# HGRN products moved from GpSimd to VectorE, operand tiles placed anew, and the opening, norm factors and row copies reordered

## The chip, the cores and the metric

The kernel runs on one core of a Trainium2 chip. The metric is the time of one execution on the device in microseconds (us); the median of several runs is compared. A difference is measured against the same runs of the kernel before.

## What is computed

The reference passes 256 tokens of 1024 features through two networks, one after the other, all in float32. The first is one block: a norm, a mixer with four branches and gates, a norm, a feed-forward, and a final norm. The second has two layers: a norm, HGRN, a feed-forward; a norm, an LRU mixer, a feed-forward; and a final norm. Cut to what matters here:

```
h = rmsnorm(x, norm_mix);  x = x + hybrid_mixer(h, ...)
h = rmsnorm(x, norm_ffn);  x = x + (silu(h @ w_gate) * (h @ w_up)) @ w_down
x = rmsnorm(x, norm_final)
x = x + hgrn2_mixer(rmsnorm(x, ...), ...);  x = x + swiglu_2(rmsnorm(x, ...), ...)
x = x + rglru_mixer(rmsnorm(x, ...), ...);  x = x + swiglu_2(rmsnorm(x, ...), ...)
x = rmsnorm(x, norm_final_2)

hgrn2_mixer: q = silu(proj_q);  f = lb + (1 - lb) * sigmoid(fl);  k = (1 - lb) * sigmoid(-fl)
             S_t = diag(f_t) S_{t-1} + k_t v_t^T;  o_t = S_t^T q_t     (8 heads of 128)
```

Here `lb` is a softmax over two rows of a parameter, the floor of the forget gate.

## The kernel before

**Matmuls.** Every dense product is done in three passes (`mm3`, line 152). Each operand is split into a high and a low part: `split` (line 99) casts a tile to the reduced form on ScalarE (line 100) and takes the difference on VectorE (line 101). The three passes are high by high (L154), and the two mixed ones (L155, L156). Weights come by DMA into `raw`, four tiles of 1 MB that SyncE's queue fills, and are split into `whi` and `wlo`, 1024 columns at a time. Activations, transposed, are split into `hh` and `hl` (the normed input of each stage), `ah` and `al` (the inner width of a feed-forward), `yh` and `yl` (branches), `oh` and `ol` (HGRN's output), `uh` and `ul` (LRU).

There are two forms of product. `gemm_a` (line 158) keeps a 128x128 piece of the activations stationary and streams up to 512 weight columns past it; so do the feed-forwards. `gemm_b` (line 185) keeps a 128x128 piece of the weights stationary and streams the 256 tokens past it; it serves where the output is wanted transposed, in the mixer, HGRN and LRU. A feed-forward (`swiglu`, line 316) runs over 2816 inner columns, five blocks of 512 and one of 256, for gate and up, and then over the 22 blocks of `ah` for the way down.

**What sets the order.** Each engine runs its instructions in one order, which a scheduler lays out from the order of the code, the readiness of the operands and priorities. `high_priority(offset=...)` moves the weight splits ahead (line 121), `issue_after` ties a piece of work behind an instruction. Tiles of a pool are reused in turn (`bufs`), and a tile's address follows from the pools and the tiles made ahead of it.

**The norm.** `norm_input` (line 199) squares a 128x512 part of `x` on ScalarE with a running sum, transposes it, scales it and splits it into `hh` and `hl`. The factor of the norm is applied later, at the eviction: `rstd` (line 232) works it out with a power on GpSimd (line 246), and `row` (line 248) makes it a row `rrow` over the tokens with two small matmuls against `dg` (line 264) and a copy on ScalarE (line 266).

**The opening.** ScalarE has the squares and casts of four parts of `x`, the casts of the first weights, and `lru_rates` (line 570), which is passed to the first feed-forward as `aside` and whose operands are parameters alone. An activation function from another set needs a table load on ScalarE (ACT_TABLE_LOAD in the trace).

**The mixer.** `skew_bias` (line 389) builds a table of relative biases with a small matmul and copies it on GpSimd's queue to `relv` and, in two large copies, to `skew` in DRAM; `bias4` reads it back for attention. `rows4` (line 437) fetches four heads' rows for the first branch, whose loop over heads (lines 644 to 656) forms `mt` from them: two operations on VectorE, an exponential on ScalarE (L651), a product on VectorE (L652), three small matmuls.

**HGRN.** At its entry (lines 1086 to 1100) the norm factors `rf` and `r` are made, `x` is scaled by `rf` on GpSimd (L1100), and the first matmuls' results are evicted as `u` = accumulator times `rrow` on VectorE (L779, L786). `hq` is `u` times its sigmoid, on GpSimd (L782); `hk` and `hf` come from ScalarE and VectorE. Then `hgrn_scores` (line 825) forms `pr` = `hq` times `hk` (L834) and its low part `pl` (L836) on GpSimd, its high part `ph` on ScalarE, sums them with a matmul of ones, and goes through seven levels with products `G` (L876) on VectorE. Meanwhile the weights of the next matmuls are split on ScalarE and VectorE.

Of the kernel before, what the change touches and what calls it, by code (L numbers as in the profile page):

```python
# [20 lines left out]
EPS = 1e-6  # L21
NEG = -1.0e30
# [52 lines left out]
class Build:  # L75
    def __init__(self, tc, a):
        self.tc, self.nc, self.a = tc, tc.nc, a
        self.uid = 0
        self.turn = 0
        self.share = 0  # L80
        self.parts = 2
        self.hold = []
        self.burst = 0
        self.wmore = None
        self.place = -1
        self.ahead = 400
# [111 lines left out]

    def norm_input(self, x, n, t, wcol, hi, lo, ss):
# [3 lines left out]
        junk = self.tmp.tile([P, 512], F32, tag="junk", name=self.nm("junk"), bufs=1)  # L203
        if ss is not None:
            nc.scalar.activation(junk, xc, AF.Square, accum_out=ss[:, t, n:n + 1])
# [26 lines left out]
    def rstd(self, ss, scale=1.0 / D):  # L232
# [3 lines left out]
        nc.vector.tensor_tensor(r, ss[:, :, 0], ss[:, :, 1], op=ALU.add)  # L236
        self.rsqrt(r, r, scale)
# [20 lines left out]
    def make_row(self, r):  # L258
        nc = self.nc
# [5 lines left out]
        rr = self.small.tile([P, S], F32, tag="rrow", name=self.nm("rrow"))  # L265
# [20 lines left out]
    def constants(self):  # L286
# [9 lines left out]

        self.cmask = c.tile([P, 3, P], F32, name="cmask")
        nc.gpsimd.memset(self.cmask, 1.0)
        for j in (0, 2):
            nc.gpsimd.affine_select(self.cmask[:, j], self.cmask[:, j], pattern=[[1, P]], compare_op=ALU.is_ge,  # L300
                                    fill=0.0, base=0, channel_multiplier=-1)
# [14 lines left out]
    def swiglu(self, hk, r, wg, g0, wu, u0, wd, x, finish, apart=0, aside=None):  # L316

        nc = self.nc
        with self.tc.tile_pool(name=self.nm("ffn"), bufs=1) as fp:
            ah = fp.tile([P, FF // P, S], F32R, name=self.nm("ah"))  # L320
            al = fp.tile([P, FF // P, S], F32R, name=self.nm("al"))
            for c0 in range(0, FF, 512):
                if c0 == 1024 and aside:
                    aside()
                n = min(512, FF - c0)
                psg, psu = self.gemm_pair(hk, wg, g0 + c0, wu, u0 + c0, n, early=c0 == 0)
                for t in range(2):
                    sg = fp.tile([P, 512], F32, tag="sg", name=self.nm("sg"), bufs=3)
                    pr = fp.tile([P, 512], F32, tag="pr", name=self.nm("pr"), bufs=3)
                    nc.scalar.activation(sg[:, :n], psg[t][:, :n], AF.Silu, scale=r[:, t:t + 1])  # L330
# [42 lines left out]
    def mixer(self, hk, r, rr, x, finish):  # L373
        nc, a, tc = self.nc, self.a, self.tc
        w_in = a["w_in"][0]
        with tc.tile_pool(name="yT", bufs=3) as ytp, tc.tile_pool(name="att", bufs=1) as at, \
# [12 lines left out]
            def skew_bias():  # L389
# [47 lines left out]
            def rows4(h0):  # L437
                rw = mp.tile([P, 4, S], F32, tag="rows", name=self.nm("rows"), bufs=1)
# [48 lines left out]

            qT2, kT2, v2 = load_qkv(3080)
# [80 lines left out]

    def lru_rates(self):  # L570
# [35 lines left out]
    def mamba(self, hk, r, rr, w_in, mp, rows4, dtc, acol, yT, then):  # L606
# [4 lines left out]
        xins = self.conv_inputs(mp, 2)  # L611
        for b in (4, 6, 0, 2):
# [9 lines left out]
        for g in range(2):  # L622
# [5 lines left out]
            nc.vector.tensor_tensor(c, ps[:, :384], self.cmask.rearrange("p a b -> p (a b)"), op=ALU.mult)  # L628
# [119 lines left out]
    def hgrn(self, hk, r, rr, x, finish):  # L748
# [3 lines left out]
        w = a["hgrn_w_in_2"][0]  # L752
        LV = (64, 32, 16, 8, 4, 2, 1)
        with tc.tile_pool(name="hgrn", bufs=1) as hp:
            lbp = self.col["hgrn_lb_2"]
            lb = hp.tile([P, 8], F32, name="lb")
            om = hp.tile([P, 8], F32, name="om")
            lt = hp.tile([P, 2, 8], F32, name="lt")
            nc.vector.tensor_tensor(lb, lbp[:, 0:8], lbp[:, 8:16], op=ALU.max)
            for i in range(2):  # L760
                nc.vector.tensor_tensor(lt[:, i], lbp[:, i * 8:(i + 1) * 8], lb, op=ALU.subtract)
            nc.scalar.activation(lt, lt, AF.Exp)
            nc.vector.tensor_tensor(om, lt[:, 0], lt[:, 1], op=ALU.add)
            nc.vector.reciprocal(om, om)
            nc.vector.tensor_tensor(lb, lt[:, 0], om, op=ALU.mult)
            nc.vector.tensor_tensor(om, lt[:, 1], om, op=ALU.mult)
            v = hp.tile([P, 2, D], F32, name="hv")
            gs = hp.tile([P, 2, D], F32, name="hg")
            oh = [hp.tile([P, 4, S], F32R, name=f"oh{g}") for g in range(2)]
            ol = [hp.tile([P, 4, S], F32R, name=f"ol{g}") for g in range(2)]  # L770
            qkf = []
            for g in range(2):
                q, k, f = (hp.tile([P, 4, S], F32, tag=n, name=self.nm(n), bufs=2) for n in ("hq", "hk", "hf"))
                qkf.append((q, k, f))
                for c in range(2):
                    h0 = 4 * g + 2 * c
                    for i, ps in enumerate(self.gemm_b(hk, w, h0 * P, 2)):
                        u = hp.tile([P, S], F32, tag="u", name=self.nm("u"), bufs=3)
                        nc.vector.tensor_tensor(u, ps, rr(), op=ALU.mult)  # L779
                        sg = hp.tile([P, S], F32, tag="sgq", name=self.nm("sgq"), bufs=2)  # L780
                        nc.scalar.activation(sg, u, AF.Sigmoid)
                        nc.gpsimd.tensor_tensor(q[:, 2 * c + i], u, sg, op=ALU.mult)  # L782
                    for i, ps in enumerate(self.gemm_b(hk, w, D + h0 * P, 2)):
                        h = h0 + i
# [241 lines left out]
    def body(self):  # L1026
        nc, a, tc = self.nc, self.a, self.tc
        with ExitStack() as es:
# [28 lines left out]
            for n in range(2):  # L1057
                for t in range(2):
                    finish(n, t)
# [103 lines left out]
```

## Time and profile before

| | us |
|---|---|
| median of 3 runs | 1179.6 |
| lowest and highest | 1176.96 and 1179.66 |
| the profiled execution | 1177.61 |
| its span, first to last instruction | 1175.9 |
| mean granted clock of TensorE | 0.992 of full speed |

The span is 1.7 us shorter than the execution's own time. The profile lists busy time by engine, groups of instructions by line and tile, and what each engine waited for; a timeline gives single instructions with their start in us from the span's start. The ends of matmuls are modelled, their starts are recorded. TensorE's granted clock is given for any stretch: 1.00 is 2.4 GHz, 0.50 is 1.2 GHz.

### The profile page before, as it was taken

What the parts mean: (1) busy time and instruction counts of PE and PEld (TensorE: products, weight loads), DVE (VectorE), ACT (ScalarE), POOL (GpSimd) and SP (SyncE); (2) the same over time, 40 slices, a digit from 0 to 9 for tenths busy, and PEclk for the clock granted to TensorE, in tenths of its full rate; (3) what the DMA queues carried; (4) which work ended last, traced back from release to release, by engine and by line L of the source; (5) the groups of instructions that cost most, each with busy time, mean ns of one, the idle gap of its engine ahead of it and who ended that gap; (6) DMA issues with size and microseconds to landing.
All of it is one profiled execution on the core that took longest, in us unless ns stands there. A gap on an engine that the chain in (4) does not pass through costs nothing.

```text
span 1175.9 us, 15771 instructions
## 1 busy us (share of the span) xinstructions
PE 1140.0 (97%) x6308; PEld 981.0 (83%) x6308; DVE 737.0 (63%) x971; ACT 615.5 (52%) x909; POOL 82.1 (7%) x87
## 2 busy tenths in 40 slices
PE   7999999999999999998999999999999879999997
PEld 7899897888888888888989878888889778888886
DVE  6976555566575555556898676555458767555552
ACT  6646647654455444446542465444446876444441
POOL 1100010000000000006520140000000000000000
PEclk9999999999999999999999999999999989999999
DMA  9785245446555555456353337554554536555440
GB/s 299 188 265 190 87 144 188 162 147 206 184 192 184 181 186 186 172 179 204 112 179 108 108 108 251 183 195 177 197 167 156 179 120 214 185 179 179 163 159 36
DMA packets 120761, 202.78 MB, mean 172 GB/s; under 512 B 4244, under 2 KB 44437, under 8 KB 120688
## 3 DMA queue, kind: packets, MB, share of 16 engines
q1 hardware_dynamic: 117264, 192.59, 50.0%
q0 software_dynamic: 2992, 8.56, 2.6%
q8 instruction: 49, 0.80, 0.3%
q10 hardware_dynamic: 432, 0.63, 0.2%
q14 instruction: 24, 0.20, 0.0%
HBM read 200.64 MB, written 4.25 MB: 174 GB/s over the span
## 4 chain that ended last, share of the span: by engine, by line
PE 84%; ACT 6%; DVE 5%; DMA 3%; issue 2%; POOLq 0%; POOL 0%; SPq 0%; ACTq 0%; DVEq 0%
PE acc L154 25%; PE acc L156 25%; PE acc L155 25%; DMA raw<-in_w_in_dram 2%; DVE wlo L101 2%; PE tp L274 2%; PE tp L865 2%; ACT whi L100 2%; PE tp L695 1%; PE tp L208 1%; DVE G L876 1%; PE tp L724 1%; PE tp L732 0%; DMA rows<-acd 0%; PE tp L731 0%
## 5 line engine op out<-in xcount | busy, mean ns | idle before, releaser
L101 DVE TENSOR_TENSOR wlo<-raw,whi 128x1024 fp32r<-128x1024 f32 (+3 forms) x364 | 444.2, 1225 | 303.5 <-ACT whi L100 296.9
L100 ACT CAST whi<-raw 128x1024 fp32r<-128x1024 f32 (+3 forms) x372 | 382.0, 1033 | 363.2 <-PE acc L156 294.3
L156 PE MATMUL acc<-whi,hl 128*128 128x512 f32 (+2 forms) x832 | 316.2, 381 | 0.0
L155 PE MATMUL acc<-wlo,hh 128*128 128x512 f32 (+2 forms) x832 | 313.7, 377 | 1.3 <-DVE wlo L101 1.3
L154 PE MATMUL acc<-whi,hh 128*128 128x512 f32 (+2 forms) x832 | 311.3, 378 | 1.3 <-ACT whi L100 1.1
L155 PEld LDWEIGHTS acc<-wlo,hh 128*128 128x128 f32 x832 | 156.4, 188 | 31.0 <-DVE wlo L101 2.4
L154 PEld LDWEIGHTS acc<-whi,hh 128*128 128x128 f32 x832 | 156.3, 188 | 28.7 <-ACT whi L100 1.9
L156 PEld LDWEIGHTS acc<-whi,hl 128*128 128x128 f32 x832 | 156.4, 188 | 28.1 <-issue 0.7
L154 PE MATMUL acc<-hh,whi 128*128 128x256 f32 (+1 forms) x496 | 142.2, 289 | 9.5 <-ACT rg L951 4.5
L156 PE MATMUL acc<-hh,wlo 128*128 128x256 f32 (+1 forms) x496 | 141.6, 287 | 1.9 <-DVE wlo L101 1.9
L155 PE MATMUL acc<-hl,whi 128*128 128x256 f32 (+1 forms) x496 | 141.8, 287 | 0.3 <-DVE hl L101 0.3
L154 PEld LDWEIGHTS acc<-hh,whi 128*128 128x128 f32 (+1 forms) x496 | 95.7, 194 | 12.7 <-ACT rg L951 4.7
L155 PE MATMUL acc<-wlo,ah 128*128 128x512 f32 x264 | 103.1, 391 | 0.0
L156 PE MATMUL acc<-whi,al 128*128 128x512 f32 x264 | 102.6, 389 | 0.0
L154 PE MATMUL acc<-whi,ah 128*128 128x512 f32 x264 | 102.5, 390 | 0.0
L156 PEld LDWEIGHTS acc<-hh,wlo 128*128 128x128 f32 (+1 forms) x496 | 95.6, 193 | 2.8 <-DVE wlo L101 2.6
L155 PEld LDWEIGHTS acc<-hl,whi 128*128 128x128 f32 (+1 forms) x496 | 95.8, 193 | 1.3 <-DVE hl L101 0.6
L156 PEld LDWEIGHTS acc<-whi,al 128*128 128x128 f32 x264 | 49.6, 188 | 10.2
L154 PEld LDWEIGHTS acc<-whi,ah 128*128 128x128 f32 x264 | 49.6, 188 | 10.1
L155 PEld LDWEIGHTS acc<-wlo,ah 128*128 128x128 f32 x264 | 49.6, 188 | 10.1
L100 ACT CAST ah<-tp 128x512 fp32r<-128x512 f32 (+1 forms) x36 | 19.8, 550 | 33.9 <-PE tp L274 33.9
L330 ACT ACTIVATE sg<-acc,rstd 128x512 f32<-128x512 f32 (+1 forms) x36 | 23.3, 648 | 20.4 <-PE acc L156 20.4
(306 smaller groups left out, 1250.8 us busy)
## 6 DMA issues: line engine op xcount, KB each, us to landing
raw<-in_ffn_w_in_dram SPq DMA_DIRECT2D x44, 1024.0 KB, 5.2
raw<-in_w_in_dram SPq DMA_DIRECT2D x33, 1024.0 KB, 5.1
raw<-in_ffn_w_out_dram SPq DMA_DIRECT2D x20, 1024.0 KB, 5.1
raw<-in_hgrn_w_in_dram SPq DMA_DIRECT2D x16, 1024.0 KB, 5.5
raw<-in_w_ffn_gate_dram SPq DMA_DIRECT2D x11, 1024.0 KB, 5.1
raw<-in_w_ffn_up_dram SPq DMA_DIRECT2D x11, 1024.0 KB, 5.2
raw<-in_w_ffn_down_dram SPq DMA_DIRECT2D x10, 1024.0 KB, 5.1
raw<-in_w_branch_dram SPq DMA_DIRECT2D x8, 1024.0 KB, 5.1
```

What stands on the lines that cost most here:

```text
L100: self.nc.scalar.copy(hi, src)
L101: (eng or self.nc.vector).tensor_tensor(lo, src, hi.bitcast(F32), op=ALU.subtract)
L154: mm(ps, sh, mh, start=start, stop=False)
L155: mm(ps, sh, ml, start=False, stop=False)
L156: mm(ps, sl, mh, start=False, stop=stop)
L208: last = nc.tensor.transpose(ps[:, j * P:(j + 1) * P], xc[:, j * P:(j + 1) * P], self.ident)
L274: nc.tensor.transpose(ps[:, j * P:(j + 1) * P], src[:, j * P:(j + 1) * P], self.ident)
L330: nc.scalar.activation(sg[:, :n], psg[t][:, :n], AF.Silu, scale=r[:, t:t + 1])
L695: nc.tensor.matmul(ps[par][:, jj * W:(jj + 1) * W], qT[pr, 2 * gi + jj, qt * P:(qt + 1) * P], kT(2 * gi + jj)[pr, :W], start=True, stop=True)
L724: nc.tensor.transpose(ps[:, i * P:(i + 1) * P], sp[:, i, b * P:(b + 1) * P], self.ident)
L865: nc.tensor.matmul(ps[:, c:c + 64], k[:, h, ts], q[:, h, ts].rearrange("p (n u l) -> p n u l", u=2, l=L)[:, :, 1], start=True, stop=True)
L876: nc.vector.tensor_tensor(G2, G[:, :, 0], G[:, :, 1], op=ALU.mult)
```

## The change

Six things change. (1) The tiles of `hh` and `hl` become 128 elements longer, and their contents start at an offset: STILL (96 elements) where they are stationary, in the feed-forwards, MOVING (16) for the three mixers. Other tiles shift with pools: `cmask` leaves the constants, `oh` and `ol` are the first in HGRN's pool, a tile of 32 elements that nobody uses is put into LRU's. (2) HGRN's `hq`, `pr` and `pl` go from GpSimd to VectorE, `x` times `rf` to ScalarE. (3) The opening writes the squares after the four transposes and casts. (4) `aside` is tied behind a silu of the first feed-forward, and the floors of HGRN (`hgrn_floors`) are worked out there too. (5) The factors of the norm and their row get a priority (`rush`). (6) In the mixer the copies to `skew` are written in two places, and `rows` has two buffers in place of one.

```diff
+STILL, MOVING = 96, 16
...
-    def new_h(self):
-        hi = [self.hp.tile([P, 4, S], F32R, tag=f"hh{n}", name=self.nm("hh")) for n in range(2)]
-        lo = [self.hp.tile([P, 4, S], F32R, tag=f"hl{n}", name=self.nm("hl")) for n in range(2)]
+    def new_h(self, place):
+
+
+        def part(tag):
+            t = self.hp.tile([P, 4 * S + 128], F32R, tag=tag, name=self.nm(tag[:2]))
+            return t[:, place:place + 4 * S].rearrange("p (k s) -> p k s", s=S)
+
+        hi, lo = ([part(f"{u}{n}") for n in range(2)] for u in ("hh", "hl"))
...
-        nc.vector.tensor_tensor(r, ss[:, :, 0], ss[:, :, 1], op=ALU.add)
-        self.rsqrt(r, r, scale)
+        with self.tc.high_priority(offset=self.rush):
+            nc.vector.tensor_tensor(r, ss[:, :, 0], ss[:, :, 1], op=ALU.add)
+            self.rsqrt(r, r, scale)
...
                 if c0 == 1024 and aside:
-                    aside()
+                    with self.tc.issue_after(last.ins):
+                        aside()
...
-                for g in range(2):
-                    nc.gpsimd.dma_start(skew[g], relv[:, g].unsqueeze(1).to_broadcast([8, P, NV]))
+                copies(0)
+
+            def copies(g):
+
+                nc.gpsimd.dma_start(skew[g], relv[:, g].unsqueeze(1).to_broadcast([8, P, NV]))
...
-                rw = mp.tile([P, 4, S], F32, tag="rows", name=self.nm("rows"), bufs=1)
+                rw = at.tile([P, 4, 384], F32, tag="sp", name=self.nm("rows"), bufs=2)[:, :, :S]
...
+            copies(1)
             qT2, kT2, v2 = load_qkv(3080)
...
-                        nc.gpsimd.tensor_tensor(q[:, 2 * c + i], u, sg, op=ALU.mult)
...
+                        nc.vector.tensor_tensor(q[:, 2 * c + i], u, sg, op=ALU.mult)
...
+            qkf = [made(g) for g in range(2)]
+            for t in range(2):
+                nc.scalar.activation(x[:, t], x[:, t], AF.Copy, scale=rf[:, t:t + 1])
...
-        nc.gpsimd.tensor_tensor(pr, q.rearrange("p h t -> p (h t)"), k.rearrange("p h t -> p (h t)"), op=ALU.mult)
-        nc.scalar.copy(ph, pr)
-        nc.gpsimd.tensor_tensor(pl, pr, ph.bitcast(F32), op=ALU.subtract)
+        nc.vector.tensor_tensor(pr, q.rearrange("p h t -> p (h t)"), k.rearrange("p h t -> p (h t)"), op=ALU.mult)
+        self.split(ph, pl, pr)
...
             xins = self.conv_inputs(lp, 4)
+            lp.tile([P, 32], F32, name="apart")
...
-            begin(col["norm_mix"])
+            begin(col["norm_mix"], MOVING)
             for n in range(2):
                 for t in range(2):
-                    finish(n, t)
+                    self.norm_input(x, n, t, state["w"], state["hi"], state["lo"], None)
+            for n in range(2):
+                for t in range(2):
+                    self.square(x[:, t, n * 512:(n + 1) * 512], state["ss"][:, t, n:n + 1])
...
-            for t in range(2):
-                nc.gpsimd.tensor_scalar(x[:, t], x[:, t], rf[:, t:t + 1], None, op0=ALU.mult)
-            begin(col["norm_ffn_2"][:, 0:8])
+            begin(col["norm_ffn_2"][:, 0:8], STILL)
```

ScalarE in the opening, before and after. `junk` is a square, `lam` and `c` belong to `lru_rates`, `whi` of 320 columns is the first weight:

```order
L584 ACTIVATE lam_3636<-lam_3636 128x8
L205 ACTIVATE junk_120,ss_104<-x 128x512
L100 CAST hh_105<-tsc_116 128x4x128
L586 ACT_TABLE_LOAD
L586 ACTIVATE c_3634<-lam_3637 128x8
L205 ACTIVATE junk_131,ss_104<-x 128x512
L100 CAST hh_105<-tsc_127 128x4x128
L205 ACTIVATE junk_142,ss_104<-x 128x512
L100 CAST whi_177<-raw_175 128x320
```

```order
L427 ACTIVATE sm<-pcol 40x1
L204 ACTIVATE junk_143,ss_100<-x 128x512
L102 CAST hh_101<-tsc_110 128x4x128
L204 ACTIVATE junk_145,ss_100<-x 128x512
L102 CAST hh_101<-tsc_119 128x4x128
L204 ACTIVATE junk_147,ss_100<-x 128x512
L102 CAST whi_173<-raw_171 128x320
```

The two activations of `lru_rates` and their table load are gone; squares and casts alternate as before.

ScalarE in the mixer, at the second pair of heads, before and after. `mt` are the exponentials, `whi` the casts of the weights:

```order
L100 CAST whi_904<-raw_898 128x1024
L100 CAST whi_962<-raw_960 128x1024
L651 ACT_TABLE_LOAD
L651 ACTIVATE mt_683<-mt_683 128x384
L651 ACTIVATE mt_691<-mt_691 128x384
L100 CAST whi_966<-raw_960 128x1024
```

```order
L102 CAST whi_903<-raw_897 128x1024
L686 ACT_TABLE_LOAD
L686 ACTIVATE mt_682<-mt_682 128x384
L686 ACTIVATE mt_690<-mt_690 128x384
L102 CAST whi_961<-raw_959 128x1024
L102 CAST whi_965<-raw_959 128x1024
```

The first cast of the next weight tile has moved behind the table load and the two exponentials. On GpSimd's queue the second `rows` now follows the first, ahead of `relv`, `skew` and the first `bias`; before, it came last of these. The matmul that `relv` waits for stands at row 227 of TensorE's order, before at 179.

VectorE in HGRN, where the first group's products begin, before and after:

```order
L779 TENSOR_TENSOR u_5114<-acc_5064,rrow_4826 128x256
L876 TENSOR_TENSOR G_5394<-hf_4757 128x512
L876 TENSOR_TENSOR G_5438<-G_5394 128x256
L876 TENSOR_TENSOR G_5466<-G_5438 128x128
L876 TENSOR_TENSOR G_5494<-G_5466 128x64
L101 TENSOR_TENSOR wlo_5199<-raw_5196,whi_5198 128x1024
L876 TENSOR_TENSOR G_5522<-G_5494 128x32
L779 TENSOR_TENSOR u_5119<-acc_5089,rrow_4826 128x256
L845 TENSOR_TENSOR hq_4755<-hq_4755,hf_4757 128x1024
L101 TENSOR_TENSOR wlo_5203<-raw_5196,whi_5202 128x1024
```

```order
L902 TENSOR_TENSOR G_5394<-hf_4783 128x512
L861 TENSOR_TENSOR pr_5367<-hq_4781,hk_4782 128x1024
L815 TENSOR_TENSOR hq_5077<-u_5140,sgq_5142 128x256
L902 TENSOR_TENSOR G_5438<-G_5394 128x256
L103 TENSOR_TENSOR wlo_5225<-raw_5222,whi_5224 128x1024
L871 TENSOR_TENSOR hq_4781<-hq_4781,hf_4783 128x1024
L812 TENSOR_TENSOR u_5145<-acc_5115,rrow_4852 128x256
L902 TENSOR_TENSOR G_5466<-G_5438 128x128
L103 TENSOR_TENSOR pl_5369<-pr_5367,ph_5368 128x1024
L103 TENSOR_TENSOR wlo_5229<-raw_5222,whi_5228 128x1024
```

`pr`, `hq` and `pl` now stand between the weight differences. At HGRN's entry ScalarE's order has the two instructions of `x` times `rf` between the first and the second cast of a weight tile, both ahead of the copy of `rrow`; before, the casts and `rrow` followed one another.

## Rows read from the trace of the kernel before

**Rows 1.** The page's first part: busy us, share of the span, instructions of each engine.

```profile
PE 1140.0 (97%) x6308; PEld 981.0 (83%) x6308; DVE 737.0 (63%) x971; ACT 615.5 (52%) x909; POOL 82.1 (7%) x87
```

**Rows 2.** Waits of TensorE, whole run: what for, us in total, times, longest.

```profile
PE acc L154 <- ACT rg L951: 5.3, 2, 4.5
PE acc L154 <- ACT uh L100: 4.0, 1, 4.0
```

**Rows 3.** Timeline of TensorE, (a) to (d): start, us, operation, tiles.

```profile
402.15 0.39 PE L154 MATMUL acc<-whi,hh 128*128 128x512 f32 x1
...
420.94 0.40 PE L155 MATMUL acc<-wlo,hh 128*128 128x512 f32 x1
...
483.03 0.40 PE L156 MATMUL acc<-whi,al 128*128 128x512 f32 x1
...
511.60 0.40 PE L156 MATMUL acc<-whi,al 128*128 128x512 f32 x1
...
672.75 0.39 PE L155 MATMUL acc<-wlo,oh 128*128 128x512 f32 x1
...
680.65 0.39 PE L156 MATMUL acc<-whi,ol 128*128 128x512 f32 x1
...
469.23 0.28 PE L154 MATMUL acc<-whi,hh 128*128 128x256 f32 x1
...
476.53 0.28 PE L156 MATMUL acc<-whi,hl 128*128 128x256 f32 x1
```

**Rows 4.** Timeline of ScalarE and TensorE in the opening; idle time before in brackets.

```profile
6.74 1.28 ACT L586 ACT_TABLE_LOAD   x1
...
9.89 0.44 ACT L100 CAST whi<-raw 128x320 fp32r<-128x320 f32 x1
...
10.39 0.43 PE L154 MATMUL acc<-hh,whi 128*40 128x256 f32 x1 [2.02 <-ACT whi L100]
```

**Rows 5.** The mixer: timelines of ScalarE and TensorE, then a window's busy times, clock.

```profile
68.55 1.05 ACT L100 CAST whi<-raw 128x1024 fp32r<-128x1024 f32 x1 [5.51 <-DMA raw<-in_w_in_dram]
...
72.08 0.43 PE L654 MATMUL tp<-xc,mt 128*128 128x64 f32 x2 [1.26 <-DVE mt L652]
...
74.30:77.40 3.10, 3.10 (x16) 3.10 (x16) 2.12 (x8) 2.19 (x4) 0.00 (x0) 0.50 0.94 302
```

**Rows 6.** Timelines of GpSimd, VectorE and TensorE at HGRN's entry.

```profile
551.99 5.68 POOL L1100 TENSOR_SCALAR x<-x,rf 128x1024 f32<-128x1024 f32 x2
...
552.12 2.05 DVE L101 TENSOR_TENSOR wlo<-raw,whi 128x1024 fp32r<-128x1024 f32 x1 [0.90 <-ACT whi L100]
...
554.57 0.38 PE L154 MATMUL acc<-hh,whi 128*128 128x256 f32 x1 [2.70 <-DVE u L779]
```

**Rows 7.** HGRN's products: timelines of VectorE and GpSimd; waits of TensorE, 555 to 612.

```profile
563.11 1.21 DVE L101 TENSOR_TENSOR wlo<-raw,whi 128x1024 fp32r<-128x1024 f32 x1
...
570.61 2.85 DVE L876 TENSOR_TENSOR G<-hf 128x512 f32<-128x512 f32 x1
...
574.84 3.44 DVE L101 TENSOR_TENSOR wlo<-raw,whi 128x1024 fp32r<-128x1024 f32 x1
...
579.77 1.75 DVE L101 TENSOR_TENSOR wlo<-raw,whi 128x1024 fp32r<-128x1024 f32 x1
...
581.52 0.68 DVE L856 TENSOR_TENSOR p<-hq,hk 128x512 f32<-128x512 f32 x1
...
598.84 2.07 DVE L876 TENSOR_TENSOR G<-hf 128x512 f32<-128x512 f32 x1
...
601.61 3.44 DVE L101 TENSOR_TENSOR wlo<-raw,whi 128x1024 fp32r<-128x1024 f32 x1
...
574.80 2.39 POOL L836 TENSOR_TENSOR pl<-pr,ph 128x1024 fp32r<-128x1024 f32 x1 [0.75 <-ACT ph L835]
...
PE acc L156 <- DVE wlo L101: 1.9, 2, 1.6
PE acc L155 <- DVE wlo L101: 0.8, 1, 0.8
```

More of the change, by code (lines that the diff above doesn't have):

```diff
@@ L85, in __init__ @@
         self.place = -1
+        self.rush = 600
         self.ahead = 400
@@ L196, in block_b, with square @@
         return ps
+    def square(self, xc, out):
+        junk = self.tmp.tile([P, 512], F32, tag="junk", name=self.nm("junk"), bufs=1)
+        self.nc.scalar.activation(junk, xc, AF.Square, accum_out=out)
     def norm_input(self, x, n, t, wcol, hi, lo, ss):
@@ L202, in norm_input @@
         xc = x[:, t, n * 512:(n + 1) * 512]
-        junk = self.tmp.tile([P, 512], F32, tag="junk", name=self.nm("junk"), bufs=1)
         if ss is not None:
-            nc.scalar.activation(junk, xc, AF.Square, accum_out=ss[:, t, n:n + 1])
+            self.square(xc, ss[:, t, n:n + 1])
         ps = self.tp()
@@ L258, in make_row, with row_of @@
     def make_row(self, r):
+        with self.tc.high_priority(offset=self.rush):
+            return self.row_of(r)
+    def row_of(self, r):
         nc = self.nc
@@ L264, in make_row @@
             nc.tensor.matmul(ps[:, t * P:(t + 1) * P], self.ones, dg, start=True, stop=True)
-        rr = self.small.tile([P, S], F32, tag="rrow", name=self.nm("rrow"))
+        rr = self.small.tile([P, S], F32, tag="rrow", name=self.nm("rrow"), bufs=1)
         nc.scalar.copy(rr, ps[:, :S])
@@ L295, in constants @@
         nc.vector.tensor_copy(self.ones_r, self.ones)
[L297 to L301, printed above, removed]
         self.col = {}
@@ L568, in mixer, with hgrn_floors @@
             gp.__exit__(None, None, None)
+    def hgrn_floors(self):
+        nc = self.nc
+        self.floors = lb, om = [self.const.tile([P, 8], F32, name=n) for n in ("lb", "om")]
+        lbp = self.col["hgrn_lb_2"]
+        lt = self.small.tile([P, 2, 8], F32, tag="lt", name="lt", bufs=1)
+        nc.vector.tensor_tensor(lb, lbp[:, 0:8], lbp[:, 8:16], op=ALU.max)
+        for i in range(2):
+            nc.vector.tensor_tensor(lt[:, i], lbp[:, i * 8:(i + 1) * 8], lb, op=ALU.subtract)
+        nc.scalar.activation(lt, lt, AF.Exp)
+        nc.vector.tensor_tensor(om, lt[:, 0], lt[:, 1], op=ALU.add)
+        nc.vector.reciprocal(om, om)
+        nc.vector.tensor_tensor(lb, lt[:, 0], om, op=ALU.mult)
+        nc.vector.tensor_tensor(om, lt[:, 1], om, op=ALU.mult)
     def lru_rates(self):
@@ L611, in mamba @@
         xins = self.conv_inputs(mp, 2)
+        cmask = mp.tile([P, 3, P], F32, name="cmask")
+        nc.gpsimd.memset(cmask, 1.0)
+        for j in (0, 2):
+            nc.gpsimd.affine_select(cmask[:, j], cmask[:, j], pattern=[[1, P]], compare_op=ALU.is_ge,
+                                    fill=0.0, base=0, channel_multiplier=-1)
         for b in (4, 6, 0, 2):
@@ L745, in attention, with hgrn @@
             self.to_T(y[:, t], yT[0], yT[1], t)
-    def hgrn(self, hk, r, rr, x, finish):
+    def hgrn(self, hk, r, rr, rf, x, finish):
         nc, a, tc = self.nc, self.a, self.tc
         w = a["hgrn_w_in_2"][0]
+        lb, om = self.floors
         LV = (64, 32, 16, 8, 4, 2, 1)
         with tc.tile_pool(name="hgrn", bufs=1) as hp:
[L755 to L766, printed above, removed]
+            oh = [hp.tile([P, 4, S], F32R, name=f"oh{g}") for g in range(2)]
+            ol = [hp.tile([P, 4, S], F32R, name=f"ol{g}") for g in range(2)]
@@ L1046, in body, with begin @@
             state = {}
-            def begin(wcol):
+            def begin(wcol, place):
                 state["ss"] = self.stat()
-                state["hi"], state["lo"], state["hk"] = self.new_h()
+                state["hi"], state["lo"], state["hk"] = self.new_h(place)
                 state["w"] = wcol
@@ L1062, in body @@
             hk = state["hk"]
-            begin(col["norm_ffn"])
+            begin(col["norm_ffn"], STILL)
             self.mixer(hk, r, rr, x, finish)
@@ L1068, in body @@
             nc.vector.tensor_tensor(wc, col["norm_final"], col["norm_mix_2"][:, 0:8], op=ALU.mult)
-            begin(wc)
+            begin(wc, MOVING)
             wfs = ExitStack()
@@ L1110, in body @@
             rr = self.row(r)
-            begin(col["norm_ffn_2"][:, 8:16])
+            begin(col["norm_ffn_2"][:, 8:16], STILL)
             self.ahead = 150
```

72 lines of the change are left out of this document (35 added, 37 removed).

## The prediction

> **What bounds the kernel now.** The first part of the profile's page comes first: TensorE is busy 97% of the span, VectorE 63%, ScalarE 52%, GpSimd 7% [rows 1]. So a microsecond off TensorE's stream is a microsecond off the end, and work on another engine counts only where TensorE waits for it. Next the waits of TensorE: the two largest groups, 5.3 us for `rg` and 4.0 us for `uh`, lie in the LRU mixer [rows 2]. The change leaves that code as it is, so they stay. What is left is small: the waits in the stretches below, and the rate of the matmuls themselves. That rate is read from starts, not from the durations of the table, which are modelled. In [rows 3] four unbroken stretches, all at the full granted clock, give the first and the last start: (a) 83 matmuls of a 512-column weight tile against stationary `hh`/`hl` in the first feed-forward, 18.79 us for 82 steps, 229.1 ns a step; (b) 127 of the same shape against `ah`/`al`, 28.57 us for 126 steps, 226.7 ns; (c) 35 against `oh`/`ol`, 7.90 us for 34 steps, 232.4 ns; (d) 63 of 256 columns against `hh`/`hl`, 7.30 us for 62 steps, 117.7 ns. Half of (b) would be 113.4 ns.
>
> **What the four stretches have in common and what not.** Instruction, shape, clock and the source of the moving tile are the same in (a), (b) and (c). The place of the stationary tile in SBUF isn't. In the program built from the kernel before, weights start at byte 416 of a 512-byte period, `ah`/`al` at 416, `hh`/`hl` at 96, `oh`/`ol` at 32. Same offset as the weights: 226.7; the two other offsets: 229.1 and 232.4. In the changed program weights, `ah`/`al`, `oh`/`ol` and the `hh`/`hl` of the feed-forwards (STILL) all start at 32; the `hh`/`hl` that serve as moving operand in the mixers (MOVING) start at 224, as far from the weights (192) as before. The trace shows the rates; that the difference of offsets is their cause is my reading, and I choose it because no other feature I could find sorts the stretches.
>
> **Part 1, the offsets.** Three feed-forwards have 480 matmuls of 512 columns each against `hh`/`hl` (five blocks of 512, 8 K-steps, 2 halves, 3 passes, gate and up): 1440 x 2.4 ns = 3.5 us. Their last blocks have 256 columns: 288 x (117.7 - 113.4) = 1.2 us. `oh`/`ol`: 96 x 5.7 = 0.5 us. Sum 5.2 us, all of it on TensorE's stream, where nothing hides it. `uh`/`ul` move from one untried offset to another (288 against 32); 96 matmuls, at most the 4.3 ns of (d) either way, 0.4 us, taken as 0. Bounds: 0 if offsets mean nothing, 5.6 with `uh`. The Trainium skill speaks against this term: "SBUF — State Buffer", section "SBUF: two separate sides", has TensorE wait for nobody at SBUF, only VectorE and GpSimd contending. By it the places would be worth nothing; the three rates in [rows 3] are not explained by it.
>
> **Part 2, the opening.** Before, ScalarE runs the logarithm of `lru_rates` between the first casts, with a table load of 1.28 us at 6.74 [rows 4]; the cast of the first weights comes at 9.89 and the first dense matmul at 10.39, after a wait of 2.02 us. `lru_rates` is now tied behind a silu in the first feed-forward, so this load leaves the opening, and 0.3 us of tiny activations with it. The order shows that the squares, though written after the casts, still stand between them, so the squares bring nothing. In the other direction the second halves of `hh` come close behind the first dense matmuls, so a few tenths may be waited for again. Taken: -1.2 us, bounds -0.3 and -1.6. The moved loads fall into the first feed-forward, beside ScalarE at half load; if that cover were gone each costs its 1.28 us. The HGRN floors move the same way; they were beside other work, and count as 0.
>
> **Part 3, the mixer.** GpSimd's queue held `rows` of the second head group behind a bias copy that waits for the skew copies; it now stands ahead of them. On ScalarE, the exponentials of `mt` stood behind a weight cast that waited 5.51 us for its load, at 68.55 [rows 5]; then TensorE waited 1.26 us at 72.08 for `mt`, and the clock was granted at half (1.2 GHz) from 74.3 to 77.4. In the new order table load and exponentials stand ahead of that cast. So the 1.26 us should go. The half clock costs 1.55 us of these 3.1 us, if it goes too. Against it: the matmul that starts `relv` and `skew` stands 48 rows later on TensorE, some 5.7 us at the 118 ns of (d), so the copies now collide with later weight loads, and the cast may then be late for its own matmuls. Bounds -2.8 and +2.0 (the 1.26 us back, and 0.7 more of the 5.51 us); taken -0.8.
>
> **Part 4, the entry of HGRN.** `x` times `rf` leaves GpSimd, where two took 5.68 us from 551.99, beside a weight difference on VectorE that took 2.05 us [rows 6] where 1.21 is usual [rows 7]. It saves 0.84 us on the path to `u`, for which TensorE waited 2.70 us. But on ScalarE it now stands ahead of a weight cast and of `rrow`, without which no `u` can start: two of 128x1024 at the 1.05 us of the cast in [rows 5] are 2.1 us, and they wait for the power on GpSimd. How much of them lies in the time that ScalarE was idle anyway I can't read off exactly; queued behind it are the cast, `rrow`, then `u` on VectorE, then TensorE. Bounds -0.8 and +1.3; taken +0.2.
>
> **Part 5, the HGRN products.** While GpSimd forms `pl` (2.39 us at 574.80), a weight difference on VectorE that starts at 574.84 takes 3.44 us instead of 1.21; G takes 2.85 and 2.07 where the same form takes 0.68 [rows 7]. What VectorE loses in these rows: 2.17 + 2.23 + 0.54 + 1.39 + 2.23 = 8.6 us. What it gains as work: `pr` and `pl` of two groups, 4 x 1.21 = 4.8, and eight `hq` of 128x256, 0.41 each by halving the step from 0.68 to 1.21 once more (an estimate), 3.3: 8.1 us. So the load stays, net about -0.5, but no weight difference is held for 3.4 us any more. TensorE waited there 1.9 and 0.8 us for `wlo` [rows 7]. In the new order `wlo` number three of the stretch has G, `pr` and one `hq` in front, 2.3 us against the 2.85 of G alone before, and its own 1.21 instead of 3.44; the next one has `pl` directly ahead. Both come earlier than before by more than the 1.6 us waited. Taken -2.5, bounds -2.7 (all) and +1.0, if `pl` waits for ScalarE's cast with two weight differences behind it.
>
> **Sum.** -5.2 - 1.2 - 0.8 + 0.2 - 2.5 = -9.5 us. The profiled execution took 1177.6 us (span 1175.9); the runs shown have median 1179.6 and lowest 1177.0. I set the base between, 1178.5, and get **1169.0 us**.
>
> **Rivals.** (B) The offsets do nothing (the skill's rule named above gives this): only the waits go, -4.3, 1174.2 us. For it: the steps are 1% apart, and the cause is argued; against: dozens of stretches of (a) and (b) through the whole run have the same two values. (C) The waits only change place: VectorE, as loaded in this stretch as before by the sum above, keeps TensorE waiting as before, and the mixer's cast comes late; -1.2 - 5.2 + 0 + 1.0 + 0.2 = -5.2, 1173.3 us. (D) Slower: not the distance between the operands counts but the place itself, and 32 is the slow one (it has the 232.4 of `oh`). Then all stationary tiles go to 232.4: 1440 x 3.3 = 4.8, and the 1176 matmuls against `ah`, `yh`, `sh` and `loh`, now at 226.7, lose 5.7 each, 6.7; with the waits' -4.3 that is +7.2, 1185.7 us. It decides once the mean loss over these 2616 matmuls passes 1.6 ns, since 2616 x 1.6 ns is the 4.3 us that the waits give. For it: nothing in the trace parts distance from place. Against: as moving operand, `hh` at 96 costs nothing against weights at 416, though as stationary it does, so the place alone is not the rule. (E) The change doesn't do what it says in the opening: that the squares keep their place is in the sum already.
>
> **Chances.** Forecast 0.60; B 0.15; C 0.15; D 0.07; the rest 0.03. A difference under about 0.3%, 3.5 us, can't be told from none. B and C lie at the edge of it, about two thirds of them beyond: faster 0.77, same 0.14, slower 0.09. The range takes in B and C and their half-clock variants upward, 1177, and downward all gains at their bounds, -5.6 - 1.6 - 2.8 - 0.8 - 2.7 = -13.5, and some 3 us if a half-clock stretch in HGRN goes as well: 1162.
>
> **What would show it.** Right: starts 226.7 ns apart for `hh` in the feed-forwards and for `oh`, 113.4 in the last blocks; the first dense matmul at about 9.2; no row of a VectorE product above 1.3 us between 565 and 612, and no wait for `wlo` there above 0.5; no wait for `mt` near 70. Wrong: `ah` slower than 226.7 (D), `hh` still 229 (B), new waits for `wlo` or `whi` in HGRN or at 70 to 80 (C), or a wait for `u` of over 3.5 us at HGRN's entry.

## The result, and the profile after

The changed kernel takes 1171.9 us (median of 4 runs, 1169.9 to 1172.1) against 1178.9 us before: ratio 0.9939, 95% interval 0.9922 to 0.9956. It is faster, by 7 us where 9.5 had been forecast, and within the range. The profiled spans, 1170.4 and 1175.9 us, differ by 5.5 us. Where they part is read from the starts of the same matmuls in both traces:

| stretch before, us | difference, us |
|---|---|
| 0 to 10.4, to the first dense matmul | -1.8 |
| 10.4 to 41.5, first part of the mixer | -1.3 |
| 41.5 to 98.1, heads of the first branch | -3.7 |
| 98.1 to 203.3, rest of the mixer's projections | +1.6 |
| three feed-forwards | -0.6, -0.6, -0.5 |
| 537.9 to 666.9, HGRN's entry, products and first output | +1.6 |
| LRU and the rest | -0.2 |

So most of the gain lies in the first 100 us, and HGRN as a whole lost. Within HGRN the entry (to 554.6) takes 0.3 us more, the products (to 593.0) 2.6 less, and the rest to 666.9 takes 3.9 more. The boundary at 41.5 shifts 0.7 us of work: four small matmuls (`bcT`) stand ahead of it after and behind it before, so at equal work the two stretches that it parts gained about 2.0 and 3.0 us.

First the steps that answer to [rows 3], in the timeline of TensorE after (start, us): 83 matmuls of 512 columns against `hh`/`hl`, 35 against `oh`/`ol`, 63 of 256 columns against `hh`/`hl`.

```profile
374.03 0.40 PE L156 MATMUL acc<-whi,hh 128*128 128x512 f32 x1
...
392.66 0.40 PE L157 MATMUL acc<-wlo,hh 128*128 128x512 f32 x1
...
668.89 0.40 PE L157 MATMUL acc<-wlo,oh 128*128 128x512 f32 x1
...
676.61 0.39 PE L158 MATMUL acc<-whi,ol 128*128 128x512 f32 x1
...
463.40 0.28 PE L156 MATMUL acc<-whi,hh 128*128 128x256 f32 x1
...
470.83 0.28 PE L158 MATMUL acc<-whi,hl 128*128 128x256 f32 x1
```

That is 227.2 ns a step (229.1 before), 227.1 (232.4) and 119.8 (117.7). The first two went nearly as forecast (226.7), the third the other way. Next the waits of TensorE, whole run (us in total, times, longest), then timelines: TensorE at the first dense matmul, and ScalarE, VectorE and TensorE at HGRN's entry and exit:

```profile
PE acc L156 <- ACT rg L978: 5.7, 2, 4.5
PE tp L290 <- DVE on L931: 5.7, 2, 4.3
PE acc L156 <- DVE u L812: 3.3, 1, 3.3
PE acc L158 <- DVE wlo L103: 0.6, 2, 0.5
...
8.59 0.31 PE L156 MATMUL acc<-hh,whi 128*40 128x256 f32 x1 [0.52 <-ACT whi L102]
...
544.28 2.19 ACT L829 ACTIVATE x<-x,rf 128x1024 f32<-128x1024 f32 x2 [0.41 <-POOL rf L258]
546.37 1.03 ACT L102 CAST whi<-raw 128x1024 fp32r<-128x1024 f32 x1
547.31 0.36 ACT L282 COPY rrow<-tp 128x256 f32<-128x256 f32 x1
...
565.13 0.69 DVE L902 TENSOR_TENSOR G<-hf 128x512 f32<-128x512 f32 x1
565.73 1.22 DVE L861 TENSOR_TENSOR pr<-hq,hk 128x1024 f32<-128x1024 f32 x1
...
653.62 1.06 PE L921 MATMUL tp<-hv,st 128*128 128x128 f32 x8
658.97 0.84 PE L290 MATMUL tp<-ident,on 128*128 128x128 f32 x4 [4.30 <-DVE on L931]
```

The waits for `wlo` in HGRN's products and for `mt` are gone (the 0.6 us for `wlo` lies in the opening), `G` takes 0.69 us where it took 2.85 [rows 7], and a wait that before had not existed, 4.3 us for `on`, stands at HGRN's exit. `on` is the normed output; TensorE has nothing between the state matmuls and its transposition. TensorE's timeline before and its order, before and after, say why. Before, 24 dense matmuls stood there; after, none does:

```profile
658.03 1.06 PE L895 MATMUL tp<-hv,st 128*128 128x128 f32 x8
658.84 0.48 PE L154 MATMUL acc<-whi,hh 128*128 128x512 f32 x1
...
664.20 0.39 PE L156 MATMUL acc<-whi,hl 128*128 128x512 f32 x1
664.43 0.60 PE L274 MATMUL tp<-ident,on 128*128 128x128 f32 x4
```

```order
L895 MATMUL tp_5750<-hv,st_5366 128x128 x4
L154 MATMUL acc_5872<-whi_5910,hh_3296 128x512
L155 MATMUL acc_5872<-wlo_5911,hh_3296 128x512
```

```order
L158 MATMUL acc_5873<-whi_5914,hl_3298 128x512
L907 MATMUL tp_5597<-hq_5077,hk_5078 128x128 x4
L921 MATMUL tp_5750<-hv,st_5366 128x128 x4
L290 MATMUL tp_5766<-ident,on_5763 128x128 x4
```

Three half-clock stretches of the trace after (window, TensorE, its weight loads, VectorE, ScalarE, GpSimd, clock, DMA share, GB/s): the one at 74 before is gone, the one at HGRN's entry stayed, the two others are new. Those in LRU and at the very end stand in both traces.

```profile
181.40:184.80 3.40, 3.40 (x9) 2.67 (x8) 1.99 (x3) 2.96 (x5) 0.00 (x0) 0.50 0.63 192
550.00:553.30 3.30, 3.30 (x18) 3.30 (x17) 1.99 (x7) 1.26 (x4) 0.63 (x1) 0.50 0.96 299
659.30:662.60 3.30, 3.30 (x17) 3.30 (x16) 0.75 (x1) 0.69 (x1) 0.00 (x0) 0.50 0.16 56
```

### The profile page after: what moved, and what is told of

It is laid out like the page before. It is cut to its first block, busy times and chain, and to the rows that moved or that the text cites. A ratio compares the mean times of both kernels' runs of the same rounds, so it can differ in the third digit from the quotient of the medians.

```text
span 1170.4 us, 15756 instructions
## 1 busy us (share of the span) xinstructions
PE 1134.7 (97%) x6308; PEld 980.7 (84%) x6308; DVE 732.9 (63%) x983; ACT 618.7 (53%) x911; POOL 57.1 (5%) x73
## 4 chain that ended last, share of the span: by engine, by line
PE 90%; ACT 5%; issue 2%; DVE 1%; POOL 1%; DMA 0%; POOLq 0%; ACTq 0%; DVEq 0%
PE acc L156 27%; PE acc L158 27%; PE acc L157 27%; PE tp L290 2%; PE tp L891 2%; ACT whi L102 1%; PE tp L730 1%; PE tp L214 1%; POOL wlo L103 1%; PE tp L759 1%; DVE wlo L103 1%; PE tp L767 0%; PE tp L765 0%; PE tp L766 0%; ACT av L987 0%
## 5 line engine op out<-in xcount | busy, mean ns | idle before, releaser
L103 DVE TENSOR_TENSOR wlo<-raw,whi 128x1024 fp32r<-128x1024 f32 (+3 forms) x364 | 438.0, 1209 | 293.0 <-ACT whi L102 285.9
```

The costliest lines, as they stand in the source:

```text
L103: (eng or self.nc.vector).tensor_tensor(lo, src, hi.bitcast(F32), op=ALU.subtract)
```

## The experiments

The base is the changed kernel unless an edit says otherwise. A single time is of one execution; where a ratio stands, it is to the kernel before on the same chip. The runs were made in three groups on three chips, with the kernel before beside each: its median was 1178.0 us beside e1 to e4, 1176.2 beside e5 to e8, 1177.4 beside e9 to e11. Single times from different groups are therefore compared to about 2 us only; what follows goes by stretches of the traces.

**e1_offsets: is it the distance?**

```diff
-            begin(col["norm_ffn"], STILL)
+            begin(col["norm_ffn"], 80)
-            begin(col["norm_ffn_2"][:, 0:8], STILL)
+            begin(col["norm_ffn_2"][:, 0:8], 112)
-            begin(col["norm_ffn_2"][:, 8:16], STILL)
+            begin(col["norm_ffn_2"][:, 8:16], 128)
```

> The changed kernel, with only the place of hh and hl in their tile altered, another one in each feed-forward: 64 bytes below the weights' offset in the first, 64 above in the second, 128 above in the third (before the change oh and ol stood 128 above the weights' offset in the 512-byte period). If the distance between stationary and streamed operand sets the rate, the third gives the 232.4 ns that oh and ol had, the first two give rates between 227.2 and 232.4 that differ from 227.2, and ah and al stay at 226.8 everywhere. If it was the place and not the distance, or something else in the changed program, the rates of the three feed-forwards don't follow oh and ol. For 256 columns, where distance 0 gave 121.1 against 117.8 before: open, noted for each distance.

Steps, each from the first and last start of an unbroken stretch of 63 to 127 matmuls. The 121.1 and 114.9 ns that the expectations name for 256 columns count in one step of 0.2 us behind a transposition; without it they are 119.8 and 113.4:

| `hh` past the weights, bytes of 512 | 512 columns, ns | 256 columns, ns |
|---|---|---|
| 0 (changed kernel) | 227.2 | 119.8 |
| 64 (second feed-forward) | 233.3 | 113.4 |
| 128 (third) | 232.4 to 233.3 | 120.0 |
| 192 (kernel before) | 229.1 | 117.7 |
| 448 (first) | 229.0 | 117.8 |

The third feed-forward's rows, 83 matmuls, and the second's last block, 63 of them:

```profile
1031.49 0.39 PE L156 MATMUL acc<-whi,hh 128*128 128x512 f32 x1
...
1050.62 0.39 PE L157 MATMUL acc<-wlo,hh 128*128 128x512 f32 x1
...
813.73 0.28 PE L156 MATMUL acc<-whi,hh 128*128 128x256 f32 x1
...
820.76 0.28 PE L158 MATMUL acc<-whi,hl 128*128 128x256 f32 x1
```

At 128 the rate is about the one that `oh` had before, also at 128. `oh` itself stands at 32 in both kernels and went from 232.4 to 227.1 when the weights moved; `ah`, moved with the weights from 416 to 32, kept 226.7 to 226.9. So it is the distance, not the place (rival D falls). The 233.3 at 64 lies above the range that was expected. And 256 columns have another best distance than 512. The period of 512 bytes is not shown: 192 and 448 lie 256 apart and give the same rates in both columns, so a period of 256 would serve as well. The time, 1176.1, is 4.2 above the changed kernel's median; in the trace the three feed-forwards take 5.0 us more, and the half clock at 181 isn't there.

**e7_moving: the same in the mixers.** On e2_exit (below), MOVING becomes 96 for the first mixer, 112 for HGRN, 80 for LRU.

> e2_exit with another place for hh and hl in each mixer, where they are the streamed operand of 256 columns and the stationary one of 512: at the weights' own offset in the first mixer, 64 bytes above in HGRN, 64 below in LRU. If distance sets the rate whatever the role, the 512-column matmuls against hh fall from 229 to 227.2 in the first mixer and are 233 in HGRN. For the 256-column ones the runs so far show 113.5 to 120 at an unchanged distance, so their rate is open; 121 in the first mixer and 115 in HGRN would follow the feed-forwards' last blocks.

At distance 0 the first mixer's 512-column steps are 226.7 ns (96 of them) where they were 228.9, and its 256-column steps 119.0 to 120.0 where they were 113.6 to 117.8 in e2_exit. In HGRN, at 64, 512 columns take 233.4 (62 of them), 256 columns 117.8 (43, and 267 further on), not 115. There the role of `hh` is the other one: counted as stationary less streamed tile, its 64 is 448, for which the table has 117.8. That proves little, since e2_exit has 117.8 too in the second of these stretches. Distance sets the 512-column rate in both stages; for 256 columns it isn't the only thing. With `hh` at the same distance, the same matmuls of HGRN's products (554.6 to 593.0 before) take 113.4 to 113.6 ns a step in some traces (before, after, e8_xlate) and 117.8 in e2_exit, 117.3 in e3_products; over some 270 steps that is 1.0 to 1.2 us. What decides between the two is open. The time, 1171.3 us, can't be set against that of e2_exit, which ran in another group.

**e2_exit: cover for the output's norm.** `gemm_a` gets `behind`, a state matmul of the first group; the code passes the fourth, where the text below says the first.

```diff
...
-                            self.mm_a(ps[ci][t], t, hk, k0 + k, ncols, wk[k])
+                            with self.tc.issue_after(behind) if behind and k0 else nullcontext():
+                                self.mm_a(ps[ci][t], t, hk, k0 + k, ncols, wk[k])
...
```

> The changed kernel, with one tie more: the last 24 dense matmuls of HGRN's second gate product (its K-steps 4 to 7) are issued behind the first matmul of the state output of group 0, as they stood in the kernel before. Theory: the 3.9 us lost at HGRN's exit come from these 24 matmuls (5.5 us) having moved ahead of the norm of the output, so that nothing covers the chain of squares, power and two products; then the wait of 4.3 us for on and the half clock at 659 go, 4 to 6 us off the span, to about 1165. Rival: VectorE is behind with its work by then, on comes late whatever TensorE does; then the wait only moves and the span stays within 1 us.

1169.1 us, ratio 0.9925 (0.9908 to 0.9941). From 593.0 to 666.9 the loss of 3.9 us became a gain of 0.6, 4.5 us by this tie: `on` is ready before its turn, and the half clock behind it is gone. VectorE wasn't late; the cover had been moved. In its place TensorE now waits 1.0 us for `hk`, which is counted in. From 537.9 to 666.9 it is 3.3 us, since the products ran at 117.8 ns in this trace, 1.2 us more than in the changed kernel's; e8_xlate has the same tie and 113.4, so the tie alone isn't the cause. The span gains 2.1 us, not the 4 to 6 expected: this trace comes 0.9 us later out of the opening, has no half clock at 181 (-1.6) and one more in LRU (+1.9 from 666.9 on).

TensorE's timeline at the exit, without a wait:

```profile
656.27 0.60 PE L291 MATMUL tp<-ident,on 128*128 128x128 f32 x4
```

**e3_products: hq, pr and pl back on GpSimd.**

```diff
...
-        nc.vector.tensor_tensor(pr, q.rearrange("p h t -> p (h t)"), k.rearrange("p h t -> p (h t)"), op=ALU.mult)
-        self.split(ph, pl, pr)
+        nc.gpsimd.tensor_tensor(pr, q.rearrange("p h t -> p (h t)"), k.rearrange("p h t -> p (h t)"), op=ALU.mult)
+        self.split(ph, pl, pr, nc.gpsimd)
```

> The changed kernel with hq, pr and pl back on GpSimd (x times rf stays on ScalarE). If VectorE was held by GpSimd there: weight differences of about 3.4 us beside pr and pl return, and with them waits for wlo of 2 to 3 us between 560 and 610. If the products' move also caused the new order at the exit: the 24 dense matmuls stand behind the first state matmuls again, and the wait of 4.3 us for on is gone. Both together: span 1168 to 1170; if only the first, 1173.

Both came: span 1167.1 (1168.8 us), a little below the expected 1168, and this trace has no half clock at 181. VectorE's and GpSimd's timelines and TensorE's waits, 550 to 612:

```profile
563.71 2.69 DVE L902 TENSOR_TENSOR G<-hf 128x512 f32<-128x512 f32 x1
...
594.57 3.44 DVE L103 TENSOR_TENSOR wlo<-raw,whi 128x1024 fp32r<-128x1024 f32 x1
...
594.48 2.44 POOL L103 TENSOR_TENSOR pl<-pr,ph 128x1024 fp32r<-128x1024 f32 x1 [1.16 <-ACT ph L102]
...
PE acc L158 <- DVE wlo L103: 1.1, 1, 1.1
PE acc L157 <- DVE wlo L103: 0.8, 1, 0.8
```

From 537.9 to 666.9 it takes 0.2 us more than before. So the move of the products costs 1.4 us as it stands (+1.6 against +0.2), and is worth 1.9 us with the exit covered (-1.8 in e2_exit against +0.2, rounded). The second comparison is at nearly equal rates of the 256-column matmuls, 117.8 and 117.3 ns. The first isn't: the changed kernel has 113.4 there, about 1.0 us less, so at equal rates the move would cost about 2.4 us as it stands (an estimate).

**e8_xlate: x times rf out of the entry's way.** On e2_exit:

```diff
...
             for t in range(2):
-                nc.scalar.activation(x[:, t], x[:, t], AF.Copy, scale=rf[:, t:t + 1])
+                with tc.issue_after(self.lastk):
+                    nc.scalar.activation(x[:, t], x[:, t], AF.Copy, scale=rf[:, t:t + 1])
...
```

> e2_exit with x times rf tied behind the last sigmoid of group 1, so that at HGRN's entry ScalarE casts the weights and copies rrow without it. Theory: the two products (2.2 us) ahead of the cast made u late; the wait for u falls from 3.3 to about 1.5 to 2.0 us, 1.3 to 1.8 us off the stretch from 538 to 593 and perhaps a half-clock stretch of 1.7 us with it: 1166 to 1168. Rival: the cast waits for its weight buffer anyway, rrow comes no earlier, and the time stays at that of e2_exit, 1169.

1164.6 us (1164.4 to 1165.0), ratio 0.9898 (0.9880 to 0.9915): better than both kernels. The wait for `u` is 2.2 us where it was 3.3, and the entry is 1.1 us shorter than in e2_exit: half of the 2.2 us that the two products take, for the cast now starts behind an idle time of 1.5 us. From 537.9 to 666.9 it is 2.3 us; the other 1.2 are the products' 113.4 ns in place of 117.8, which no edit here explains. The half clock at the entry stayed. ScalarE and TensorE at the entry:

```profile
543.93 1.04 ACT L102 CAST whi<-raw 128x1024 fp32r<-128x1024 f32 x1 [1.49 <-POOL mask L802]
544.88 0.37 ACT L283 COPY rrow<-tp 128x256 f32<-128x256 f32 x1
...
PE acc L156 <- DVE u L813: 2.2, 1, 2.2
```

**e6_tail: another distance for the last blocks.** On e8_xlate, `whi` of the last 256 columns starts 112 elements later in its tile in two feed-forwards.

> e8_xlate, and in the second and third feed-forward the high weights of the last 256 columns start 448 bytes further on in their tile, so that hh stands 64 bytes above them in the period. e1_offsets showed 114.9 ns at that distance for 256 columns, 121.1 at none. Theory: the passes against whi in these two blocks (128 matmuls) fall from 121.1 to about 115, 0.8 us in all, within what can't be told by the time alone but can by the starts. Rival: the rate at 256 columns goes by the tile's place or its neighbours; then it stays at 118 to 121.

The steps of the third feed-forward's last block fell from 119.8 to 117.7 ns, less than forecast, though more than nothing; 1164.3 us (1163.9 to 1165.1) can't be told from e8_xlate. `wlo` stayed where it was.

**e4_opening: aside without its tie.**

```diff
                 if c0 == 1024 and aside:
-                    with self.tc.issue_after(last.ins):
-                        aside()
+                    aside()
```

> The changed kernel without the tie of aside behind a silu: the logarithm of lru_rates and the floors may run in the opening again. If that table load made the first dense matmul late, it comes at about 10 us in place of 8.6, and the span grows by 1.2 to 1.8 us. If the first weights or x came earlier for another reason, the first dense matmul stays at 8.6 to 9.

The first dense matmul came at 10.3, and the span is 1177.8, 7.4 us more than with the tie. Only 1.7 of it is the opening: 1.9 are lost from there to 41.5, and 5.1 to 98.1, where the cast again stands ahead of the exponentials and TensorE waits 2.7 us for `mt` (some 0.7 of these 5.1 are the `bcT` matmuls, which stand behind the boundary at 41.5 here, as before). The expected range was far too small. Four runs tell what the mixer owes to which edit.

**e5_tie: the kernel before with the tie alone.** The edit of e4_opening the other way round, in the kernel before.

> The kernel before with one edit of the change alone: aside (lru_rates) tied behind a silu of the first feed-forward. Theory from e4_opening: this tie is what brings the first 100 us forward, by the table load that leaves the opening, by the clock that is granted earlier, and by the new order of ScalarE in the mixer (exponentials ahead of the cast that waits for its load), 6 to 7 us in all; then the first dense matmul comes at 8.6 to 9.0, the wait for mt and the half clock at 74 are gone, and the time is 1171 to 1173. Rival: the mixer's 5 us need the second rows buffer and the priorities of the norm factors too; then only the opening's 2 to 3 us are gained, 1175 to 1176.

Median 1175.0, but 1171.6 to 1179.1 in ten runs; ratio 0.9987 (0.9972 to 1.0002): it can't be told from the kernel before, and the theory's 1171 to 1173 is missed. In the trace, one of the faster runs (1173.5), the opening is much as in the changed kernel (first dense matmul at 9.1), while the wait for `mt` stays at 1.4 us; without a half clock behind it the stretch from 41.5 to 98.1 is still 1.3 us shorter than before at equal work.

**e11_tierush: the tie and the priorities, in the kernel before.**

```diff
...
-        nc.vector.tensor_tensor(r, ss[:, :, 0], ss[:, :, 1], op=ALU.add)
-        self.rsqrt(r, r, scale)
+        with self.tc.high_priority(offset=600):
+            nc.vector.tensor_tensor(r, ss[:, :, 0], ss[:, :, 1], op=ALU.add)
+            self.rsqrt(r, r, scale)
...
```

> The kernel before with two edits of the change: aside tied behind a silu, and the priority of the norm factors and their row (in rstd and make_row). In the built order these two together put the exponentials of the second pair of heads ahead of the cast that waits for its load; the tie alone doesn't. Theory: then the wait for mt near 70 is gone, the half clock behind it too, and the first 100 us are 6 to 7 us shorter, as in the changed kernel: 1169 to 1171 on a base of 1176 to 1178. Rival: the second rows buffer is what lets the exponentials run; then the wait for mt stays, and the time is that of e5_tie, 1175.

1181.0 us (1174.7 to 1183.8 in ten runs), ratio 1.003 (1.0012 to 1.0048): 0.3% slower than before. The theory fell. The exponentials of heads 2 and 3 are early, at 62.15, and then the next heads wait for `rows`. GpSimd, VectorE and TensorE:

```profile
63.55 0.82 POOL L455 DMA_DIRECT2D bias<-skew  x1 [19.16 <-DMA skew<-relv]
64.35 0.57 POOL L445 DMA_DIRECT2D rows<-acd  x1
...
73.72 0.35 DVE L655 TENSOR_SCALAR mt<-rows,tcol 128x256 f32<-128x256 f32 x1 [6.96 <-DMA rows<-acd]
...
75.58 0.68 PE L660 MATMUL tp<-xc,mt 128*128 128x64 f32 x2 [4.23 <-DVE mt L658]
```

**e10_rows: the changed kernel with one rows buffer.**

```diff
-                rw = at.tile([P, 4, 384], F32, tag="sp", name=self.nm("rows"), bufs=2)[:, :, :S]
+                rw = mp.tile([P, 4, S], F32, tag="rows", name=self.nm("rows"), bufs=1)
```

> The changed kernel with one buffer for rows, as before the change. On GpSimd's queue the second rows then stands behind the first bias copy again. Theory: the order on ScalarE keeps the exponentials of heads 2 and 3 ahead of the cast, so nothing is lost up to there; the later heads (4 to 7) wait for rows, as they did before without TensorE waiting; 1171 to 1172. Rival: with the earlier start TensorE now waits for the later mt, 1 to 4 us between 70 and 85.

The rival held: 2.7 us of waiting for `mt`, the half clock behind it at 76.9, and the stretch from 41.5 to 98.1 is 4.7 us longer than in the changed kernel; 1177.0 us.

**e9_rush: the changed kernel with rush at 0.**

> The changed kernel with the priority (rush) set to 0, all else kept, the second rows buffer too. The built order has the cast ahead of the exponentials again. Theory: the wait for mt of 1.3 to 2.7 us returns, and in some executions the half clock behind it: 2 to 5 us more than the changed kernel, 1173 to 1177. Rival: rows comes early by its second buffer and the wait stays away; then 1171 to 1172.

Here too the rival held: 0.2 us of waiting for `mt`, 0.6 us more than the changed kernel in that stretch, 1172.9 us. So in the mixer the gain needs the tie and the second `rows` buffer together. At equal work the stretch is 1.5 us longer than before without the tie (e4_opening) and 1.7 longer without the buffer (e10_rows), where both together save 3.0. The priorities add 0.6; on the kernel before with the tie but without the buffer (e11_tierush) they lead into the next wait, and the stretch is 4.4 longer.

## Why the prediction was right, and where its steps were not

The sign, the range and most of the size were right; the terms were not as even as the sum. That the total came so near is in part luck: in the traces 8.5 us are missing from the forecast (3.0 at the offsets, 3.9 at HGRN's exit, 1.6 at 181), and about 4.8 were gained beyond it (0.6 in the opening, 2.0 behind it, 2.2 in the mixer). One reading of [rows 2] was incomplete, without consequence: TensorE's second largest wait is 4.4 us for `x` at the start, before the 4.0 for `uh`, and the change leaves it too (4.3).

- **Offsets, -5.2 forecast, about -2.2 measured.** The mechanism is shown for 512 columns by e1_offsets and e7_moving. The size was off twice: 1.9 ns a step in place of 2.4 (the rate of `ah`, 226.7, isn't quite reached), and the last blocks of 256 columns lost 2.1 ns a step, 0.6 us in all, where 1.2 us were to be won. The step that failed was to take the best distance for 512 columns as the best for 256 too: the goal of 113.4 ns is reached at 64 bytes in e1_offsets, not at 0.
- **Opening, -1.2 forecast, -1.8 measured, and -1.3 behind it (2.0 at equal work) that I had not counted.** The wait between the transposes and the dense matmuls fell from 2.0 to 0.5 us. In the trace before, matmuls of 256 columns follow one another at 213 ns, the step of the half clock at 74.3, until 16.06; after, at 117 ns from 9.59. In the eleven traces without the long wait these slow steps end between 9.5 and 13.3 us; in the two with it (before, and e4_opening with 1.7 us) they end at 16.1 and 14.8. So the clock tends to come up sooner without the wait, but the opening alone doesn't set when: its code is the same in the changed kernel, in e10_rows (12.1) and in e2_exit (13.3). In e2_exit the stretch to 41.5 is still 0.8 us shorter than before, so the clock is only a part of this gain; the rest is not placed.
- **Mixer, -0.8 forecast, -3.7 measured in its stretch, -3.0 at equal work.** That is the wait of 1.26 us and the half clock, whose slow steps cost 1.7 us, a little over the 1.55 in the bound of -2.8; both went. What I set against them, a collision of the copies with later weight loads, cost TensorE nothing there. I named both edits, the queue on GpSimd and the order on ScalarE, but put the gain on the order. e10_rows shows that without the second buffer the wait comes back, e4_opening that without the tie it does too; e9_rush, with the cast ahead of the exponentials again, keeps most of the gain. The +1.6 further on is the half clock at 181.4; it stands in four of the traces (the changed kernel, e9, e10, e11) and not in the others, behind waits of 1.1 and 0.5 us that all thirteen traces have. What decides it is open.
- **HGRN's entry, +0.2 forecast, +0.6 measured in the wait for `u` (2.7 to 3.3), +0.3 in the stretch.** The queue was the one named: x times rf, the cast, `rrow`, `u`. e8_xlate, which takes both new rows of ScalarE out of the way, wins 1.1 us: half of their 2.2 was on the path.
- **HGRN's products, -2.5 forecast; -1.9 where the exit is covered (e2_exit against e3_products), +1.4 as the change has them.** The waits for `wlo` went as forecast, and the stretch of the products alone (554.6 to 593.0) is 2.6 us shorter; the 3.9 us at the exit were not forecast. This is the step that was missing: I followed what VectorE's order did between 565 and 612, and not what the same move did to TensorE's order at the end of the stage, where it could have been read. Rival C had the kind, a wait that changes place, but looked for it on VectorE in the same stretch.

The runs differ by 7 us, the traces by 5.5: the profiled execution of before, 1177.6, lies 1.3 us under its median, that of after, 1172.1, 0.2 above. Over all runs before ranges from 1173 to 1180.

## What to carry to other kernels

When work moves between engines in a scheduled kernel, compare the order of the bound engine over the whole stage, its end above all: the dense matmuls that cover a chain can be scheduled away from it, and one tie brings them back (4.5 us at the exit here). A step that is brought forward only gains as far as the next queue lets it: the tie and the priorities together made the kernel 0.3% slower than before, while with the second buffer beside them the mixer has the largest gain of all stretches. And where matmuls run back to back, it pays to read their rate from starts, tile by tile, and over unbroken stretches only: 0.8% of it lay in the place of `hh`, 2.3% in that of `oh`, and one step across a break put 1.3 ns on a mean of 63.

## What the hardware showed that I had not expected

The start-to-start time of matmuls at the full granted clock depends on the distance between stationary and streamed tile. For 512 columns it is 227.2 to 233.3 ns, best at 0 of the five distances tried. For 256 columns against `hh` in the feed-forwards it is 113.4 to 120.0, best at 64 and bad at 0. The distances are counted in a period of 512 bytes; whether the period is 512 or 256, no run tells. For 256 columns in HGRN two rates, 113.4 and 117.8, come at an unchanged distance. "SBUF — State Buffer" of the Trainium skill ("SBUF: two separate sides") lets TensorE wait for nobody there; the rates in e1_offsets differ by 2.7% all the same, and the measurement decides. No run here shows what in SBUF or TensorE causes it.
